# Stick-breaking attention on one core: the second score product of a tile reads 64 rows instead of 128

## The chip, the core and the metric

The kernel runs as one launch on one core of a Trainium2 chip. The metric is the device time of the launch in microseconds. TensorE (PE in the profile; its weight loads are PEld) multiplies matrices, VectorE (DVE), ScalarE (ACT) and GpSimd (POOL) work elementwise, and SyncE (SP) issues the transfers between device memory and the core's own memory.

## The reference

One layer of an encoder: a stick-breaking attention over 2048 positions with 16 heads of 64 channels, then a SwiGLU feed-forward part of width 2816, each between RMS norms with a modulation that comes from a conditioning vector. What matters here is how the scores are made and used:

```python
qkv = (h @ w_qkv).reshape(b, s, 3, N_HEADS, HEAD_DIM)
q, k, v = qkv[:, :, 0], qkv[:, :, 1], qkv[:, :, 2]
for q0 in range(0, s, SB_BLOCK):
    end = q0 + SB_BLOCK
    z = jnp.einsum('bthd,bshd->bhts', q[:, q0:end], k[:, :end]).astype(jnp.float32) * scale
    ...
    sp = jnp.where(mask, jax.nn.softplus(z), 0.0)
    rest = lax.cumsum(sp, axis=3, reverse=True)
    log_a = jnp.where(mask, z - rest, -jnp.inf)
    a = jnp.exp(log_a).astype(v.dtype)
    outs.append(jnp.einsum('bhts,bshd->bthd', a, v[:, :end]))
```

The products are wanted in float32 precision. The kernel gets it by splitting each operand into a rounded high part and a low part, the remainder, and by adding up products of these parts.

## The kernel before, in words

**Stages.** From 0 to about 84 us the first norms and projections are made. From there to about 1391 us attention runs, interleaved with the projections of later heads. Then come the output projection and the feed-forward part; the change touches nothing in them.

**Units of attention.** Heads are taken in 8 pairs `p`, the head within the pair is `e`. Queries and keys are cut into 4 blocks of 512 positions. A unit is (`p`, `e`, query block `qb`, key block `sc`) with `sc` from `qb` down to 0, 160 units in all (L485), and each unit has four tiles `r` of 128 queries by up to 512 keys: 640 tiles. On the diagonal (`sc == qb`) a tile is only (r + 1) x 128 keys wide, so that 64 tiles each are 128, 256 and 384 wide, and the rest are 512 wide.

**Queries and keys in memory.** `project` (L376) makes keys, queries and values of a pair and a block, each as 24 products of 128 rows by 512 columns (L155 to L157), and `split` (L420) puts the high and the low part of the result beside each other into a tile `qn` or `kn`, with the pair's two heads in the two halves of the 128 rows. Transfers then arrange these for the scores. The tile `kt` holds, for each head `e`, the keys' high part in rows 0 to 63 and their low part in rows 64 to 127 (L437 to L441). The tile `qt` holds, for each head, high and low part beside each other in the free dimension, and that twice, in rows 0 to 63 and again in rows 64 to 127 (L450 to L455). One pair and block, `PARKED`, is projected early, kept in device memory and fetched back by `unpark` (L358) with the same layout.

**A score tile.** `score` (L511) makes two products into one accumulator: part 0 takes the queries' high part in all 128 rows and so adds high x high and high x low; part 1 takes the queries' low part in all 128 rows and adds low x high and low x low. The queries are the operand that is loaded (LDWEIGHTS), the keys the one that streams, up to 512 columns wide.

**What follows a tile.** `sigmoids` (L525, ScalarE) reads the accumulator twice, `break_sticks` (L541) scans it on VectorE and multiplies on GpSimd, `turn` (L565) transposes on TensorE, `split_high` and `split_low` (L575, L583) split the transposed weights, and `weigh_values` (L590) multiplies them with the values.

**Order.** TensorE, ScalarE, VectorE and GpSimd run in an order written out by hand (`ORDER_IN_SLOT`): one slot per tile, in which the values' products of the tile nine slots earlier come first, then the two score products of this tile, then one or two slices of a later projection (three products each), and in every second slot two sets of transposes. How many slices a slot gets is reckoned in advance (`RATE`, L1093 to L1097). Transfers all stand in SP's queue, in the order of the program.

Of the kernel before, what the change touches and what calls it, by code (L numbers as in the profile page):

```python
# [16 lines left out]
P = 128  # L17
# [4 lines left out]
HD = 64  # L22
# [59 lines left out]
def f32(ap):  # L82
    return ap.bitcast(F32)
# [3 lines left out]
def hybrid_trunk_kernel(  # L87
# [40 lines left out]
    q_park = dram.tile([P, 2, BT], F32, name="q_park")  # L128
# [42 lines left out]
    def sb(shape, dtype, **kw):  # L171

        return (odd if kw["tag"] in ODD_TAGS else att).tile(shape, dtype, **kw)
# [184 lines left out]
    def unpark():  # L358
        p, b = PARKED
        kt = sb([P, 2, BT], F32R, name=f"kt{p}_{b}", tag="kt", bufs=BUFS["kt"])  # L360
        for e in range(2):
            for part in range(2):
                nc.sync.dma_start(
                    f32(kt[part * HD : (part + 1) * HD, e]), k_park[e * HD : (e + 1) * HD, part]
                )
        qt = sb([P, 2, 2, BT], F32R, name=f"qt{p}_{b}", tag="qt", bufs=BUFS["qt"])
        for e in range(2):
            for half in range(2):
                nc.sync.dma_start(
                    f32(qt[half * HD : (half + 1) * HD, e]), q_park[e * HD : (e + 1) * HD]  # L370
                )
        v = sb([P, 4, 2, 2, HD], F32R, name=f"v{p}_{b}", tag="v", bufs=BUFS["v"])
        nc.sync.dma_start(f32(v), v_park)
        keys[p, b], queries[p, b], values[p, b] = kt, qt, v

    def project(at):  # L376
# [6 lines left out]
        if STEPS[at] == (PARKED[0], 1):  # L383
            unpark()
        h = norm_h[b] if p == 0 or parked else h_load(p, b)

        def product(t):
            if begun:
                return first_acc[t]
            w = weights[p, t]  # L390
            if parked and t == 1:
                acc = zps.tile([P, BT], F32, name=f"pj{p}_{b}_{t}", tag="z")
            else:
                acc = accps.tile([P, BT], F32, name=f"pj{p}_{b}_{t}", tag="acc")
            ahead = b == NB - 1 and p + 1 < NPAIR
            for k in range(KC):
                if t == 1:
                    if p == 0:
                        first_norm(b, k + 3)
                    if k == 0 and nb and nb > 1:  # L400
                        x_load(nb)
                    if k == 5 and waiting:
                        waiting.pop()()
                if parked and t == 1 and k % 2 == 0:
                    nc.sync.dma_start(*stores[k // 2])
                if parked and (t, k) == (1, 6):
                    split_early(1, 2, ["whl"])
                if t == 0 and nb:
                    (x_square if k < 4 else x_scale)(nb, k % 4)
                if t == 2 and k in (2, 4, 6):  # L410
                    first_norm(nb, k // 2 - 1)
                if ahead and k == 0:
                    load_weights(p + 1, t)
                if ahead and k == 6:
                    split_weights(p + 1, t)
                mm3(acc, (w[0][:, k], w[1][:, k]), (h[k][:, 0], h[k][:, 1]), k == 0, k == KC - 1)
                yield
            return acc

        def split(acc, tag):  # L420
            hl = sb([P, 2, BT], F32R, name=f"{tag}n{p}_{b}", tag="qkn", bufs=BUFS["qkn"])
            nc.scalar.copy(hl[:, 0], acc)
            nc.vector.tensor_tensor(hl[:, 1], acc, f32(hl[:, 0]), op=ALU.subtract)
            return hl
# [5 lines left out]
        n = split((yield from product(1)), "k")  # L430
# [13 lines left out]
        n = split((yield from product(0)), "q")  # L444
        if closing:
            wo_load(0, 3, "whl")
        if parked:
            nc.sync.dma_start(q_park, f32(n))
        else:
            qt = sb([P, 2, 2, BT], F32R, name=f"qt{p}_{b}", tag="qt", bufs=BUFS["qt"])  # L450
            for e in range(2):
                for half in range(2):
                    nc.sync.dma_start(
                        f32(qt[half * HD : (half + 1) * HD, e]), f32(n[e * HD : (e + 1) * HD])
                    )  # L455
            queries[p, b] = qt

# [35 lines left out]
    def projections():  # L493
        for at in range(len(STEPS)):
            yield from project(at)
# [15 lines left out]
    def score(i, r):  # L511

        p, e, qb, sc = units[i]
        q, k = queries[p, qb], keys[p, sc]
        diag = sc == qb
        n = (r + 1) * P if diag else BT
        z = zps.tile([P, BT], F32, name=f"z{i}_{r}", tag="z")
        for part in range(2):
            nc.tensor.matmul(  # L519
                z[:, :n], q[:, e, part, r * P : (r + 1) * P], k[:, e, :n],  # L520
                start=part == 0, stop=part == 1,
            )
        scores[i, r] = z
# [490 lines left out]
    def beside_out(b, n):  # L1014
# [40 lines left out]

    stages = {
        "score": score, "sig": sigmoids, "stick": break_sticks,
        "turn": turn, "high": split_high, "low": split_low, "av": weigh_values,
    }
# [7 lines left out]
    for s in range(4 * len(units) + last):  # L1067
        if s % 4 == 0 and s // 4 < len(units):
            p, e, qb, sc = units[s // 4]
# [327 lines left out]
    for n, (s, f) in enumerate(groups):  # L1397
# [3 lines left out]
        for at, product in enumerate(PRODUCTS):  # L1401
            acc = banks_of[{1: 0, 6: 0, 7: 0, 4: 0, 5: 1, 3: 1, 2: 2}[product]]
            for k in range(H4):
                hl, r = left[n - (n == FC), product], right[s, product, k]
# [129 lines left out]
    for m, (at, s, i) in enumerate(out_steps):  # L1534
        product = OUT_PRODUCTS[at]
        acc = bank("y", m % 4, f"o{m}")
        for g in range(GO):
            part, at_part = (0, g) if g < GQ else (1, g - GQ)
            hl, r = left_out[m][part][:, :, at_part], right_out[at, g]
# [61 lines left out]
```

## Time and profile before

| | |
|---|---|
| median of three timed runs | 2849.48 us (2848.0 to 2850.19) |
| profiled execution, its time | 2847.31 us |
| profiled execution, span from first to last instruction | 2845.1 us |
| granted TensorE clock | 0.999 |
| first and last load of the scores | 84.2 and 1391.3 us |
| products of the scores (L519) | 1280, of them 896 are 512 wide and 128 each 384, 256 and 128 wide |

The profile is taken from one execution. It lists busy time by engine; the span in 40 slices; the chain of work that ended last, followed back from the end; and groups of instructions with their count, total and mean duration, and the idle time before them. A row such as `L519 PE MATMUL z<-kt,qt 128*128 128x512 f32 x896 | 281.8, 396 | 0.0` reads: line 519, a product on TensorE into tile z from kt and qt, weights of 128 rows by 128 columns, output of 128 by 512, 896 of them, 281.8 us busy in all, 396 ns from start to modelled end of one, no idle time before them. Products overlap on TensorE, so the distance between starts is less than the duration. In the order of time, the first two columns are start and length of a group of like instructions, in us.

### The profile page before, as it was taken

Reading aid. Unit: us, or ns where it says so; the run is one execution under the profiler, and the core shown is the slowest. Engines: PE = TensorE matmul, PEld = TensorE weight load, DVE = VectorE, ACT = ScalarE, POOL = GpSimd, SP = SyncE. Lnnn points to the kernel's source line nnn. Section 1 sums busy time; section 2 is a strip of 40 time slices with the busy share of each in tenths; the row PEclk is TensorE's granted clock in tenths of the full one; section 3 lists DMA queues with packets and bytes.
Section 4 is the critical chain, followed back from the end, with each engine's and each line's share of the span. In section 5 each row is a group of like instructions: output and inputs, shape, how many; then the busy total and the mean of one; then the engine's idle time right before and its main releaser. Section 6 shows DMA issues by size and latency. Waiting matters only on the chain.

```text
span 2845.1 us, 41790 instructions
## 1 busy us (share of the span) xinstructions
PE 2795.6 (98%) x13848; PEld 2333.9 (82%) x13848; DVE 2028.4 (71%) x2822; ACT 1632.3 (57%) x3265; POOL 1277.0 (45%) x2032
## 2 busy tenths in 40 slices
PE   7999999999999999999999999999999999999998
PEld 6788888888888888887888888888788888888887
DVE  6788898888888888888866766555775665133467
ACT  5787877788787877777645533333433333322243
POOL 1475666676576655656410122221222222544454
PEclk9999999999999999999999999999999999999999
DMA  8765556656665635546289645435453335545566
GB/s 329 271 211 167 189 155 227 211 170 234 189 209 192 209 118 179 196 133 231 88 299 312 203 137 152 122 98 161 130 177 108 112 107 163 191 142 155 180 214 195
DMA packets 239368, 516.84 MB, mean 182 GB/s; under 512 B 22321, under 2 KB 110385, under 8 KB 221489
## 3 DMA queue, kind: packets, MB, share of 16 engines
q1 hardware_dynamic: 239152, 514.18, 56.0%
q8 instruction: 109, 1.79, 0.3%
q14 instruction: 107, 0.87, 0.1%
HBM read 346.85 MB, written 118.49 MB: 164 GB/s over the span
## 4 chain that ended last, share of the span: by engine, by line
PE 87%; DVE 6%; ACT 2%; DMA 2%; issue 2%; POOL 1%; SPq 0%; DVEq 0%; POOLq 0%; ACTq 0%
PE s L155 9%; PE s L156 9%; PE s L157 9%; PE z L519 8%; PE o L598 8%; PE t L570 8%; PE pj L155 6%; PE pj L156 6%; PE pj L157 6%; PE o L156 4%; PE o L157 4%; PE o L155 4%; PE y L157 2%; PE y L155 2%; PE y L156 2%
## 5 line engine op out<-in xcount | busy, mean ns | idle before, releaser
L560 POOL TENSOR_TENSOR a<-a,w 128x512 f32<-128x512 f32 (+3 forms) x640 | 619.4, 968 | 217.8 <-DVE w L553 126.8
L553 DVE TENSOR_TENSOR_SCAN w<-z,c,begin 128x512 f32<-128x512 f32 x384 | 489.6, 1279 | 81.2 <-ACT z L538 61.5
L155 PE MATMUL s<-r,l 128*128 128x512 f32 x1232 | 481.4, 391 | 4.3 <-DVE p L1364 3.7
L157 PE MATMUL s<-r,l 128*128 128x512 f32 x1232 | 479.4, 389 | 0.0
L156 PE MATMUL s<-r,l 128*128 128x512 f32 x1232 | 479.3, 389 | 0.0
L536 ACT ACTIVATE a<-z 128x512 f32<-128x512 f32 (+3 forms) x640 | 347.2, 543 | 167.2 <-PE z L519 135.7
L598 PE MATMUL o<-aT,v 128*128 128x512 f32 (+3 forms) x1280 | 384.3, 381 | 0.1
L586 DVE TENSOR_TENSOR aT<-t,aT 128x512 fp32r<-128x512 f32 (+3 forms) x640 | 359.3, 596 | 22.9 <-ACT aT L580 22.2
L519 PE MATMUL z<-kt,qt 128*128 128x512 f32 (+3 forms) x1280 | 363.1, 365 | 0.0
L580 ACT CAST aT<-t 128x512 fp32r<-128x512 f32 (+3 forms) x640 | 314.1, 533 | 73.5 <-PE t L570 63.5
L538 ACT ACTIVATE z<-z 128x512 f32<-128x512 f32 (+3 forms) x640 | 344.8, 539 | 0.0
L1372 POOL TENSOR_TENSOR one<-p,p 128x512 f32<-128x512 f32 x44 | 70.5, 1602 | 577.8 <-issue 320.5
L155 PE MATMUL pj<-ht,w 128*128 128x512 f32 x768 | 309.7, 403 | 7.6 <-ACT ht L705 2.6
L156 PE MATMUL pj<-ht,w 128*128 128x512 f32 x768 | 302.0, 393 | 1.2 <-DVE ht L710 0.7
L570 PE MATMUL t<-begin,a 128*128 128x128 f32 x2176 | 294.8, 273 | 8.5 <-DVE aT L586 7.2
L570 PEld LDWEIGHTS t<-begin,a 128*128 128x128 f32 x2176 | 255.1, 140 | 58.0 <-DVE aT L586 10.8
L157 PE MATMUL pj<-ht,w 128*128 128x512 f32 x768 | 302.1, 393 | 0.0
L155 PEld LDWEIGHTS s<-r,l 128*128 128x128 f32 x1232 | 231.3, 188 | 54.4 <-ACT l L1225 2.9
L157 PEld LDWEIGHTS s<-r,l 128*128 128x128 f32 x1232 | 231.3, 188 | 48.2
L156 PEld LDWEIGHTS s<-r,l 128*128 128x128 f32 x1232 | 231.3, 188 | 47.9 <-issue 0.5
L548 DVE TENSOR_TENSOR_SCAN w<-z,begin 128x128 f32<-128x128 f32 (+3 forms) x256 | 208.8, 818 | 75.0 <-ACT z L538 62.2
L519 PEld LDWEIGHTS z<-kt,qt 128*128 128x128 f32 x1280 | 230.3, 188 | 37.4 <-DVE w L548 0.2
(160 smaller groups left out, 4865.8 us busy)
## 6 DMA issues: line engine op xcount, KB each, us to landing
ht<-h_s SPq DMA_DIRECT2D x108, 1024.0 KB, 8.1
wi<-in_win SPq DMA_DIRECT2D x86, 512.0 KB, 4.0
qt<-qn SPq DMA_DIRECT2D x124, 256.0 KB, 4.8
ol_qt<-act_s SPq DMA_DIRECT2D x56, 512.0 KB, 3.7
act_s<-S SPq DMA_DIRECT2D x66, 256.0 KB, 4.1
br<-in_wout SPq DMA_DIRECT2D x66, 256.0 KB, 3.6
h_s<-ht SPq DMA_DIRECT2D x16, 1024.0 KB, 7.8
o_s<-os SPq DMA_DIRECT2D x128, 128.0 KB, 2.4
```

What stands on the lines that cost most here:

```text
L155: nc.tensor.matmul(acc, lhs[0], rhs[0], start=first, stop=False, **kw)
L156: nc.tensor.matmul(acc, lhs[0], rhs[1], start=False, stop=False, **kw)
L157: nc.tensor.matmul(acc, lhs[1], rhs[0], start=False, stop=last, **kw)
L519: nc.tensor.matmul(z[:, :n], q[:, e, part, r * P : (r + 1) * P], k[:, e, :n], start=part == 0, stop=part == 1,)
L536: nc.scalar.activation(a[:, :n], z[:, :n], AF.Sigmoid, scale=QK_SCALE)
L538: nc.scalar.activation(z[:, :n], z[:, :n], AF.Sigmoid, scale=-QK_SCALE)
L553: nc.vector.tensor_tensor_scan(rest[:, rev], left[:, rev], begin[:, :BT][:, rev], initial=carries[r], op0=ALU.mult, op1=ALU.bypass,)
L560: nc.gpsimd.tensor_tensor(a[:, :n], a[:, :n], rest[:, 1 : n + 1], op=ALU.mult)
L570: nc.tensor.transpose(pt[:, rb * P : (rb + 1) * P], weighed[i, rb][:, j * P : (j + 1) * P], ident)
L580: nc.scalar.copy(hl[:, 0, t0:], pt[:, t0:])
L586: nc.vector.tensor_tensor(hl[:, 1, t0:], pt[:, t0:], f32(hl[:, 0, t0:]), op=ALU.subtract)
L598: nc.tensor.matmul(acc[:, t0:], lhs, hl[:, part, t0:], start=sc == qb and j == 0 and part == 0, stop=sc == 0 and j == 3 and part == 1,)
```

## The change

The second product of each score tile (part 1, the queries' low part) reads rows 0 to 63 alone, where the keys' high part lies. It leaves out low x low, which the product of 128 rows added. Its output keeps its size. The transfers that fill rows 64 to 127 of `qt` bring the high part only, half of what they brought: in `project` from `qn`, and in `unpark` from device memory. The rest of the tile stays unwritten and unread. The line of the score products becomes L523.

```diff
@@ unpark
                 nc.sync.dma_start(
-                    f32(qt[half * HD : (half + 1) * HD, e]), q_park[e * HD : (e + 1) * HD]
+                    f32(qt[half * HD : (half + 1) * HD, e, : 2 - half]),
+                    q_park[e * HD : (e + 1) * HD, : 2 - half],
                 )
@@ project
                     nc.sync.dma_start(
-                        f32(qt[half * HD : (half + 1) * HD, e]), f32(n[e * HD : (e + 1) * HD])
+                        f32(qt[half * HD : (half + 1) * HD, e, : 2 - half]),
+                        f32(n[e * HD : (e + 1) * HD, : 2 - half]),
                     )
@@ score
-        for part in range(2):
+        for part, rows in enumerate((slice(0, P), slice(0, HD))):
             nc.tensor.matmul(
-                z[:, :n], q[:, e, part, r * P : (r + 1) * P], k[:, e, :n],
+                z[:, :n], q[rows, e, part, r * P : (r + 1) * P], k[rows, e, :n],
                 start=part == 0, stop=part == 1,
             )
```

## The prediction, as put on record before the run

> **What bounds the kernel now.** I read the page first: busy shares, clock, chain.
>
> ```profile
> span 2845.1 us, 41790 instructions
> PE 2795.6 (98%) x13848; PEld 2333.9 (82%) x13848; DVE 2028.4 (71%) x2822; ACT 1632.3 (57%) x3265; POOL 1277.0 (45%) x2032
> PEclk9999999999999999999999999999999999999999
> PE 87%; DVE 6%; ACT 2%; DMA 2%; issue 2%; POOL 1%; SPq 0%; DVEq 0%; POOLq 0%; ACTq 0%
> ```
>
> TensorE is busy for 98% of the span at an undiminished clock, and 87% of the chain that ended last is its own work. The profiled execution took 2847.31 us, so 2.2 us lie around the span; the median of the three timed runs, 2849.48, is 0.08% above it. All sums below start from 2847.31.
>
> Second, the stage that the change touches. All scores are made between 84.2 and 1391.3 us, so I asked for the busy time of each engine before, in and after that window, and then for the scores' line alone in it.
>
> ```profile
> 84.20:1391.30 1307.10, 1288.82 (x7105) 1089.73 (x7104) 1124.12 (x1466) 1029.08 (x2169) 830.62 (x1718) 1.00 0.58 187
> 84.20:1391.30 1307.10, 362.46 (x1279) 230.09 (x1280) 1.00 0.58 187
> ```
>
> The first row is PE, PEld, DVE, ACT, POOL: of 1307.1 us TensorE idles 18.3, VectorE 183.0, ScalarE 278.0. The second row is line 519: 1280 products, two for each of 640 score tiles. So a time added on TensorE here ends up in the span nearly whole, until some 183 us have been added, and beyond that too, since the other engines' work does not grow.
>
> Third, what TensorE waits for in this window (its waits, longest first).
>
> ```profile
> PE t L570 <- DVE aT L586: 7.2, 14, 1.2
> PE pj L155 <- issue: 1.4, 1, 1.4
> PE pj L155 <- DVE qn L423: 1.4, 1, 1.4
> PE xT L315 <- DVE xn L306: 1.2, 4, 0.3
> ```
>
> No transfer is in that list: TensorE never waits for the queries' copies.
>
> Fourth, the sizes of one product, from the groups of this window with shapes kept apart.
>
> ```profile
> L519 PE MATMUL z<-kt,qt 128*128 128x512 f32 x896 | 281.8, 396 | 0.0
> L156 PE MATMUL pj<-ht,w 128*128 128x512 f32 x703 | 275.7, 392 | 0.6 <-DVE ht L333 0.6
> L519 PE MATMUL z<-kt,qt 128*128 128x128 f32 x128 | 22.6, 258 | 0.0
> L519 PEld LDWEIGHTS z<-kt,qt 128*128 128x128 f32 x1280 | 230.3, 188 | 37.4 <-DVE w L548 0.2
> ```
>
> The reader is to see the "128*128": every product in this kernel, scores and all others, stands with 128 rows of weights. A score product lasts 396 ns from its start to its modelled end, and its load 188.
>
> Fifth, how these lie beside each other (order of time around 800 us, first the products, then the loads).
>
> ```profile
> 800.95 0.63 PE L519 MATMUL z<-kt,qt 128*128 128x512 f32 x2
> 801.42 0.39 PE L155 MATMUL pj<-ht,w 128*128 128x512 f32 x1
> 801.65 0.40 PE L156 MATMUL pj<-ht,w 128*128 128x512 f32 x1
> 801.88 0.39 PE L157 MATMUL pj<-ht,w 128*128 128x512 f32 x1
> 802.11 0.33 PE L598 MATMUL o<-aT,v 128*128 128x128 f32 x2
> 802.28 0.68 PE L519 MATMUL z<-kt,qt 128*128 128x512 f32 x2
> ```
>
> ```profile
> 801.19 0.19 PEld L155 LDWEIGHTS pj<-ht,w 128*128 128x128 f32 x1
> 801.42 0.19 PEld L156 LDWEIGHTS pj<-ht,w 128*128 128x128 f32 x1
> 801.65 0.19 PEld L157 LDWEIGHTS pj<-ht,w 128*128 128x128 f32 x1
> 804.25 0.30 PEld L598 LDWEIGHTS o<-aT,v 128*128 128x128 f32 x2
> ```
>
> Products 512 wide start 0.23 us apart (801.42, 801.65, 801.88) though each lasts 0.39: the next streams in while the last 0.16 of the one before is still on its way out. The load of the product that starts at 801.65 starts at 801.42, together with the product before it: loads lie wholly under streaming. Where two loads stand back to back (the 804.25 row, 0.30 for two of 0.19) the second starts 0.11 after the first, so 0.11 is what a load occupies. Two products only 128 wide take 0.17 from start to next start (802.11 to 802.28): 0.06 for the first, whose successor was already loaded, and 0.11 for the second, behind which the next load is late.
>
> **The change part by part.** No engine's order moves: the built program has the same sequence on PE, DVE, ACT and POOL, and on SP the same transfers, of which a few neighbours change places; only shapes differ.
>
> (a) The 640 second products read 64 rows of queries and keys in place of 128. Their width stays, and streaming is by width: the 128-wide products above start 0.06 apart and the 512-wide ones 0.23, a factor of four. So the products themselves save nothing: 0.
>
> (b) The upper half of the queries' tile no longer gets the low part.
>
> ```profile
> L453 SPq DMA_DIRECT2D qt<-qn x124: 461/596/2084, 52.9 to 1317.4; - x124
> qt<-qn SPq DMA_DIRECT2D x124, 256.0 KB, 4.8
> ```
>
> 62 of these 124 copies, and two of the four from the parked copy, go from 256 to 128 KB: 64 x 128 KB = 8.4 MB of the page's 517. They are still issued, at the same 0.6 us each on SP, and TensorE waited for none of them. Worth 0; the cover is that projections run ahead of the scores.
>
> (c) What is new is height. Around each second product TensorE goes from 128 rows to 64 and back: 2 x 640 = 1280 switches, each between neighbours that today overlap twice, in load and in drain. No row of before shows a product of another height, so I bound a switch from both sides. Least: slightly below 0 if a 64-row load takes less time (below, the faster rival). Most: the product before runs out fully and only then is the load begun and waited for, 0.16 + 0.19 = 0.35 us, 1280 x 0.35 = 448 us. Between them: the load no longer goes under the product before but is done in the open, 0.11, while the last 0.16 of the old product runs out beside it.
>
> I take 0.11, because it is the nearest row: where the trace does show a product whose load could not be hidden (behind a 128-wide one), the gap grew to 0.11 and not to 0.35. The sum: 1280 x 0.11 = 140.8 us. On the 64 tiles that are 128 wide (128 products in the group above) the load behind the second product is in the open already, 0.11 instead of 0.06, which takes off 64 x 0.05 = 3.2. Of the 18.3 us of idle time I count nothing as absorbed, since most of it waits for chains that move along with TensorE. 2847.31 + 137.6 = **2985 us**, 4.8% slower.
>
> Two rules of the Trainium skill bear on (c), on opposite sides. "TensorE: Matmul & The Clock Gate", section LDWEIGHTS, says that the time of a load goes by its columns and not by its rows; no run here shows 64 rows yet, and by it (a) and the loads bring nothing. "TensorEngine Tiling (Array Packing)", section Key Properties, says that "Changing tiling mode (not just tile) drains the TensorE". By that rule each switch would cost at least the run-out; this is the drain rival below, and no row of before can confirm it.
>
> (d) What is late next. If TensorE loses 0.22 us per tile, a tile's slot goes from 1307.1 / 640 = 2.04 us to 2.26. ScalarE, VectorE and GpSimd then have more slack per slot, so no new engine binds; queues and pools keep their order. No wait is added: the second score product has none of its own, and those who read the scores (ScalarE's two sigmoids) come 0.11 later per tile with slack to spare.
>
> **The rivals.**
>
> Drain: before each change of height the array runs out, then loads. For it: the trace shows two overlaps of neighbours, and a change of shape may end both. Against it: nothing shows that a load cannot run during the run-out. Price 0.16 to 0.35 per switch, 205 to 448 us: 3052 to 3295; fully in sequence 3295. Between 0.11 and 0.16 it shades into the forecast.
>
> Small bubble: only a short stop, of the order of one narrow product's 0.06 (a choice: the shortest interval between two products above): 1280 x 0.06 = 77 us, 2924, and less for a shorter one.
>
> No cost (the other side): 64 rows are just a mask on the same array, the load goes under the product before as now, and the change does in effect nothing on TensorE. It decides at zero exposed time per switch: from 5.7 us in total, 4 ns a switch, it would be slower. For it: loads are hidden today with 0.23 - 0.11 = 0.12 to spare. Time 2847.
>
> Faster: a 64-row load occupies half, 0.055. It then helps only where a load is in the open, ahead of a narrow product's successor, at most 64 x 0.055 = 3.5 us. To this comes the pair of wide scores, which takes 0.47 from start to next start (800.95 to 801.42) or 0.235 each, against 0.23: 640 x 0.005 = 3.2 us if that excess goes with the rows. Together some 7 us: 2840.
>
> **How the numbers follow.** Forecast (0.06 to 0.19 per switch, 0.19 being a whole load: 2924 to 3090) 0.34; drain above that 0.22; small bubble, up to 2924, 0.18; no cost 0.16; faster 0.10. A measurement of this kernel can tell about 0.2% from no change, 5.7 us. So slower 0.74, same 0.16, faster 0.10. Ends of the range: the high one is the full price of a switch, 3295, since the row that prices it is as real as the one I chose; the low one 2841, which takes in the no-cost case and leaves the faster one out. The likeliest case's own range is 2924 to 3090; the whole is wide because one unknown per switch is multiplied by 1280.
>
> **What would show it.** In the changed kernel the second products should stand as a form of their own with 64 rows. By the forecast, starts from a first score product to its second, and from the second to what follows, lie near 0.34 apart instead of 0.23, with the load of a switch beginning when the product before has streamed and not with it, while pairs elsewhere (three projection products in a row) stay at 0.23; the window of the scores grows by about 138 us and what follows it stays at 1453.8 (2845.1 - 1391.3). By the drain rival the starts lie 0.39 to 0.58 apart and each switch's load begins after the modelled end of the product before. By the no-cost rival the starts stay at 0.23 and the window at 1307. That only one of the two directions costs, which would halve the sum (2916), is what I would least like to have missed; the starts into and out of the 64 rows tell it. If time shows up outside the window, or on another engine, the reasoning is wrong altogether.

## The result and the profile after

The changed kernel takes 3078.47 us (median of four runs, 3076.56 to 3081.76) against 2849.05 before: ratio 1.0804, 95% interval 1.0791 to 1.0816. That is 229 us more, where 138 were forecast. The profiled execution took 3078.48 us.

The page of the changed kernel, the lines that answer to those of before:

```profile
span 3076.4 us, 41812 instructions
PE 3035.9 (99%) x13848; PEld 2314.2 (75%) x13848; DVE 2046.0 (67%) x2822; ACT 1646.1 (54%) x3265; POOL 1278.2 (42%) x2032
PEclk9999999999999999999999999999999999999999
PE 90%; DVE 4%; DMA 2%; issue 1%; ACT 1%; POOL 1%; SPq 0%; DVEq 0%; POOLq 0%; ACTq 0%
```

TensorE has the same 13848 products and 240 us more busy time at the same clock; the others have nearly what they had (VectorE 18 us more, ScalarE 14, GpSimd 1). The busy time of the loads, PEld, has not grown (2333.9 before, 2314.2 now): the loads themselves have not become longer.

The stages, cut at the first and the last score (columns as before; the last score now starts at 1620.4):

```profile
84.20:1620.00 1535.80, 1527.41 (x7105) 1069.12 (x7104) 1143.14 (x1466) 1043.18 (x2171) 831.80 (x1719) 1.00 0.48 154
1620.00:3076.40 1456.40, 1440.47 (x6405) 1188.88 (x6404) 851.31 (x1257) 556.41 (x1028) 437.48 (x295) 1.00 0.53 168
```

The scores' window has grown from 1307.1 to 1535.8 us, by 228.7, and holds the loss but for some 3 us: what follows takes 1456.4 against 1453.8. TensorE's idle time in the window has gone from 18.3 to 8.4 us: a slower TensorE waits less for its operands.

Where in the window? The groups of TensorE there, shapes kept apart; the first row is L155 before the change, the other four are the changed kernel:

```profile
L155 PE MATMUL pj<-ht,w 128*128 128x512 f32 x703 | 282.0, 401 | 5.0 <-issue 1.4 <-DVE qn L423 1.4 <-ACT hf L325 0.9
```

```profile
L155 PE MATMUL pj<-ht,w 128*128 128x512 f32 x703 | 335.5, 477 | 3.8 <-DVE qn L424 1.4 <-ACT hf L325 0.9 <-PE vt L469 0.8
L156 PE MATMUL pj<-ht,w 128*128 128x512 f32 x703 | 277.3, 394 | 0.1
L523 PE MATMUL z<-kt,qt 64*128 64x512 f32 x448 | 222.3, 496 | 0.0
L523 PE MATMUL z<-kt,qt 128*128 128x512 f32 x448 | 179.1, 400 | 0.0
```

The second score products stand as a form of their own, "64*128", and last 496 ns from start to end instead of some 400. The other row that has grown is L155, the first projection product after the scores, from 401 ns before to 477 in the mean, though nothing in it was changed; L156, one further, is as it was. Both grown rows sit right behind a change of height: in the trace 543 of the 640 second score products are followed by L155, the rest by other products of 128 rows. (The shape after the weights' is that of the operand that streams, 64 by 512 here, and not that of the output, which keeps its 128 rows.)

The loads of the same window, again L155 before the change first:

```profile
L155 PEld LDWEIGHTS pj<-ht,w 128*128 128x128 f32 x702 | 132.2, 188 | 28.7 <-DVE qn L423 1.8 <-issue 1.6 <-ACT hf L325 1.2
```

```profile
L155 PEld LDWEIGHTS pj<-ht,w 128*128 128x128 f32 x702 | 131.0, 187 | 121.0 <-issue 98.4 <-DVE qn L424 1.8 <-ACT hf L325 1.2
L523 PEld LDWEIGHTS z<-kt,qt 128*128 128x128 f32 x640 | 120.6, 188 | 19.4
L523 PEld LDWEIGHTS z<-kt,qt 64*128 64x128 f32 x640 | 117.1, 183 | 191.4 <-issue 189.7
```

A load of 64 rows takes 183 ns, as good as one of 128. But ahead of it the load unit idles, 191.4 us in 640 times, 0.30 each; ahead of the first score load of a tile it idles 0.03. Ahead of L155 the idle time has gone from 28.7 to 121.0 us. "issue" means that the profile shows nothing that it waited for: no semaphore and no transfer.

And the order of time around 900 us, products first, then loads. A group stands under the shape of its first product; the two of L523 are the one of 128 rows and the one of 64.

```profile
905.11 0.81 PE L523 MATMUL z<-kt,qt 128*128 128x512 f32 x2
905.85 0.50 PE L155 MATMUL pj<-ht,w 128*128 128x512 f32 x1
```

```profile
904.99 0.19 PEld L523 LDWEIGHTS z<-kt,qt 128*128 128x128 f32 x1
905.42 0.18 PEld L523 LDWEIGHTS z<-kt,qt 64*128 64x128 f32 x1 [0.25 <-issue]
905.85 0.19 PEld L155 LDWEIGHTS pj<-ht,w 128*128 128x128 f32 x1 [0.24 <-issue]
905.96 0.19 PEld L156 LDWEIGHTS pj<-ht,w 128*128 128x128 f32 x1
```

This is where the time goes. The first score product starts at 905.11 and has streamed by 905.34 (0.23 for 512 columns). Before the change the load of the second would have begun at about 905.11, under it. Now it begins at 905.42: not during the streaming, and not at its end either, but 0.08 after. It occupies 0.11, so the second product streams from 905.53 to 905.76; then again 0.09 pass before the projection's load begins at 905.85. The load behind that, at 905.96, lies under its predecessor as ever: 0.11 after the load before it. So each change of height costs a stop of 0.08 to 0.09 us and then a load of 0.11 in the open, 0.2 in all, in both directions alike. (A product's start is recorded when its load begins here, which is why L155 shows 0.50: load and product.)

These rows are typical. Counted from the end of streaming in the same way, the stop is 0.09 us in the median at all 1280 changes, never under 0.08, whether the product before is 128 or 512 wide and whichever line follows. From the start of a tile's first score product to the start of the second product behind the pair, the 448 tiles 512 wide take 1.085 us (median) against 0.693 before the change, 0.196 per change of height; the tiles 384 and 256 wide lose 0.39 each as well, and the tiles 128 wide 0.29. Over all 640 tiles that is 244 us. The window grew by 229, or 0.18 per change: 10 us went into idle time that TensorE had anyway, and some 5 stay open. What the stop itself is made of, no run here shows.

### The profile page after: what moved, and what is told of

The parts are those of the page before. It is cut to its first block, busy times and chain, and to the rows that moved or that the text cites. A ratio compares the mean times of both kernels' runs of the same rounds, so it can differ in the third digit from the quotient of the medians.

```text
span 3076.4 us, 41812 instructions
## 1 busy us (share of the span) xinstructions
PE 3035.9 (99%) x13848; PEld 2314.2 (75%) x13848; DVE 2046.0 (67%) x2822; ACT 1646.1 (54%) x3265; POOL 1278.2 (42%) x2032
## 4 chain that ended last, share of the span: by engine, by line
PE 90%; DVE 4%; DMA 2%; issue 1%; ACT 1%; POOL 1%; SPq 0%; DVEq 0%; POOLq 0%; ACTq 0%
PE z L523 12%; PE pj L155 9%; PE s L155 9%; PE s L157 9%; PE s L156 9%; PE o L602 8%; PE t L574 8%; PE pj L156 5%; PE pj L157 5%; PE o L155 4%; PE o L156 4%; PE o L157 4%; PE y L155 1%; PE y L157 1%; PE y L156 1%
## 5 line engine op out<-in xcount | busy, mean ns | idle before, releaser
L155 PE MATMUL s<-r,l 128*128 128x512 f32 x1232 | 482.1, 391 | 4.3 <-DVE p L1368 3.9
L523 PE MATMUL z<-kt,qt 128*128 128x512 f32 (+7 forms) x1280 | 484.9, 414 | 0.0
L156 PE MATMUL s<-r,l 128*128 128x512 f32 x1232 | 479.8, 389 | 0.0
L523 PEld LDWEIGHTS z<-kt,qt 128*128 128x128 f32 (+1 forms) x1280 | 237.7, 186 | 210.9 <-issue 189.7
L155 PE MATMUL pj<-ht,w 128*128 128x512 f32 x768 | 363.3, 473 | 6.4 <-ACT ht L709 2.6
L156 PE MATMUL pj<-ht,w 128*128 128x512 f32 x768 | 303.7, 395 | 0.8 <-DVE ht L714 0.7
L157 PE MATMUL pj<-ht,w 128*128 128x512 f32 x768 | 302.6, 394 | 0.0
L155 PEld LDWEIGHTS s<-r,l 128*128 128x128 f32 x1232 | 231.7, 188 | 54.4 <-ACT l L1229 2.9
L156 PEld LDWEIGHTS s<-r,l 128*128 128x128 f32 x1232 | 231.7, 188 | 48.5 <-issue 0.5
```

What stands on the lines that cost most here:

```text
L155: nc.tensor.matmul(acc, lhs[0], rhs[0], start=first, stop=False, **kw)
L156: nc.tensor.matmul(acc, lhs[0], rhs[1], start=False, stop=False, **kw)
L157: nc.tensor.matmul(acc, lhs[1], rhs[0], start=False, stop=last, **kw)
L523: nc.tensor.matmul(z[:, :n], q[rows, e, part, r * P : (r + 1) * P], k[rows, e, :n], start=part == 0, stop=part == 1,)
```

## The experiments

**Theory:** the price hangs on a change of height between neighbours on TensorE, about 0.18 us for each. **Rivals:** every product of 64 rows pays, whoever its neighbours are; the smaller copies cost or gain; the stop grows with the difference in height; any change of shape pays. Each ratio is to the kernel before, timed on the same chip as the run; the changes of height are counted in the traces. The two adjacent runs have 18 more than two per tile, because nine values' products and nine score products of 64 rows have no partner of their height beside them.

| run | changes of height | median us | ratio, 95% interval | us more than before, per change |
|---|---|---|---|---|
| the change | 1280 | 3078.47 | 1.0804 (1.0791 to 1.0816) | 0.179 |
| full copies | 1280 | 3076.50 | 1.0804 (1.0786 to 1.0822) | 0.178 |
| both scores 64 | 1280 | 3082.82 | 1.0818 (1.0802 to 1.0834) | 0.183 |
| 32 rows | 1280 | 3077.75 | 1.0800 (1.0784 to 1.0816) | 0.179 |
| odd tiles | 640 | 2965.93 | 1.0411 (1.0395 to 1.0426) | 0.183 |
| apart | 2560 | 3319.29 | 1.1656 (1.1636 to 1.1676) | 0.184 |
| adjacent | 1298 | 3082.08 | 1.0821 (1.0803 to 1.0839) | 0.179 |
| adjacent, upper half | 1298 | 2976.11 | 1.0444 (1.0429 to 1.0460) | - |
| 64 columns | 0 | 2846.93 | 0.9993 (0.9983 to 1.0002) | - |

**Full copies.** The height alone, the transfers as before. The edit is shown against the changed kernel.

```diff
-                    f32(qt[half * HD : (half + 1) * HD, e, : 2 - half]),
-                    q_park[e * HD : (e + 1) * HD, : 2 - half],
+                    f32(qt[half * HD : (half + 1) * HD, e]), q_park[e * HD : (e + 1) * HD]
...
-                        f32(qt[half * HD : (half + 1) * HD, e, : 2 - half]),
-                        f32(n[e * HD : (e + 1) * HD, : 2 - half]),
+                        f32(qt[half * HD : (half + 1) * HD, e]), f32(n[e * HD : (e + 1) * HD])
```

> The changed kernel with the queries' copies back at full size, so that only the height of the second product is changed. If the whole loss comes from the height: as the changed kernel, 3078 us, within 0.2%. Rival (the smaller copies cost time, by their different pieces or their place in SP's queue): nearer to 2849 us. If the smaller copies had gained something, above 3084 us.

It measured 3076.50 us, the same ratio 1.0804. The copies are worth nothing that these runs can tell, in either direction. Their rows do change: with full size there are 124 of 256 KB at 4.4 us to landing; in the changed kernel half of them are smaller and land sooner, and TensorE waits for none of them in either:

```profile
qt<-qn SPq DMA_DIRECT2D x62, 256.0 KB, 3.8
qt<-qn SPq DMA_DIRECT2D x62, 128.0 KB, 3.3
```

**Both scores 64.** Twice the products of 64 rows, as many changes of height.

```diff
-        for part, rows in enumerate((slice(0, P), slice(0, HD))):
+        for part, rows in enumerate((slice(0, HD), slice(0, HD))):
```

> Both score products of a tile take 64 rows; this leaves out the queries' high part with the keys' low part. 1280 products of 64 rows, but still only 2 changes of height per tile. Theory (a price of about 0.18 us per change of height): 3078 us, and the start of the second product comes 0.23 us after the first, its load under the first. Rival (each product of 64 rows pays, because a load of 64 rows is never done ahead): twice the loss, 2849 + 2 x 229 = 3307 us, with 0.33 us or more between the two starts.

It measured 3082.82 us, not 3307: the rival that charges each product of 64 rows falls. The loads of this run in order of time:

```profile
1201.11 0.30 PEld L602 LDWEIGHTS o<-aT,v 128*128 128x128 f32 x2
1201.78 0.29 PEld L523 LDWEIGHTS z<-kt,qt 64*128 64x128 f32 x2 [0.36 <-issue]
1202.44 0.19 PEld L155 LDWEIGHTS pj<-ht,w 128*128 128x128 f32 x1 [0.37 <-issue]
```

The two loads of 64 rows stand back to back, 0.29 for both, the second 0.11 after the first and ahead of its own product: among equals, 64 rows are loaded ahead like any others. The idle time stands before the first of them and before the projection's load, at the changes. One detail of the expectation was off: the starts of the two score products lie not 0.23 but 0.34 apart, since the first now carries the open load (0.11 + 0.23). That is the number that the rival gave as its sign, but not for the rival's reason: the second load lies only 0.11 behind the first.

**32 rows.** A larger difference in height.

```diff
-        for part, rows in enumerate((slice(0, P), slice(0, HD))):
+        for part, rows in enumerate((slice(0, P), slice(0, 32))):
```

> The second score product takes 32 rows; this leaves out the low part's products of half the channels. Theory (a fixed stop of about 0.08 us after streaming and a load of 0.11 in the open, at each change): 3078 us. Rival (the stop is the time that the difference in height takes to run out, so it grows by half from 64 to 96 rows): 0.04 more per change, 1280 x 0.04 = 51, near 3130 us. Rival (a shorter load for fewer rows): below 3050 us.

It measured 3077.75 us. Between 64 and 32 rows neither the stop nor the load depends on how far the height changes; the group of loads has 181 ns each and the same idle time ahead of them:

```profile
L523 PEld LDWEIGHTS z<-kt,qt 32*128 32x128 f32 x640 | 116.0, 181 | 192.1 <-issue 190.4
```

**Odd tiles.** Half as many changes.

```diff
-        for part, rows in enumerate((slice(0, P), slice(0, HD))):
+        for part, rows in enumerate((slice(0, P), slice(0, HD if r % 2 else P))):
```

> Only tiles 1 and 3 of a unit's four take 64 rows in the second product, copies at full size. 640 changes of height in place of 1280. Theory: half the loss, 2849 + 115 = 2964 us. Rival (part of the loss comes only when TensorE falls behind in every slot, and idle time would absorb single ones): clearly less than half, below 2940 us.

It measured 2965.93 us, half the loss within 2 us. The price is paid singly, not only by a TensorE that is late in every slot.

**Apart, and adjacent.** The sharpest pair: the second values' product is narrowed as well, and then the two score products of a tile are merely exchanged, which brings the two narrowed products together.

```diff
-        for part in range(2):
+        for part, rows in enumerate((slice(0, P), slice(0, HD))):
             nc.tensor.matmul(
-                acc[:, t0:], lhs, hl[:, part, t0:],
+                acc[:, t0:], lhs[rows], hl[rows, part, t0:],
```

> The changed kernel, and the second values' product too reads 64 of its 128 rows; this leaves out half of the weights' low part. Per slot the order is values 128, values 64, scores 128, scores 64, projection 128: four changes of height. Theory (a price per change): 2849 + 2 x 229 = 3307 us.

```diff
-        for part, rows in enumerate((slice(0, P), slice(0, HD))):
+        for part, rows in ((1, slice(0, HD)), (0, slice(0, P))):
             nc.tensor.matmul(
                 z[:, :n], q[rows, e, part, r * P : (r + 1) * P], k[rows, e, :n],
-                start=part == 0, stop=part == 1,
+                start=part == 1, stop=part == 0,
```

> The same products as the run with both narrowed, only the two of a score tile in the other order, so that per slot it goes values 128, values 64, scores 64, scores 128, projection 128: two changes of height with the same 1280 products of 64 rows. Theory (price per change): 3078 us, 229 less than with the products apart. Rival (price per product of 64 rows): the same as apart, 3307 us.

Apart 3319.29 us, adjacent 3082.08: 237 us between two kernels with the same products, the same loads and the same bytes, in another order. The exchange of the two score products takes the changes of height from 2560 to 1298, which is 0.188 us for each of the 1262 that are gone. The loads of the adjacent run show where the stops have gone:

```profile
1202.15 0.19 PEld L602 LDWEIGHTS o<-aT,v 128*128 128x128 f32 x1
1202.59 0.18 PEld L602 LDWEIGHTS o<-aT,v 64*128 64x128 f32 x1 [0.24 <-issue]
1202.69 0.19 PEld L523 LDWEIGHTS z<-kt,qt 64*128 64x128 f32 x1
1203.25 0.19 PEld L523 LDWEIGHTS z<-kt,qt 128*128 128x128 f32 x1 [0.37 <-issue]
1203.36 0.19 PEld L155 LDWEIGHTS pj<-ht,w 128*128 128x128 f32 x1
```

The stop ahead of L155 is gone (it follows 0.11 behind a load of its own height), and there is none between the two loads of 64 rows. The two that are left stand where the height changes. Whole groups say the same: 164.3 us of "issue" ahead of the values' 64 rows, 2.3 ahead of the scores' 64 rows, 189.3 ahead of the scores' 128.

```profile
L523 PEld LDWEIGHTS z<-kt,qt 128*128 128x128 f32 x640 | 119.2, 186 | 191.9 <-issue 189.3 <-DMA ht<-h_s 0.2 <-DMA kt<-kn 0.2
L523 PEld LDWEIGHTS z<-kt,qt 64*128 64x128 f32 x640 | 119.1, 186 | 3.1 <-issue 2.3 <-DVE w L552 0.4 <-DVE ht L333 0.4
L602 PEld LDWEIGHTS o<-aT,v 64*128 64x128 f32 x640 | 117.0, 183 | 173.1 <-issue 164.3 <-DVE xr L894 0.4 <-DVE x_ms L846 0.4
```

**Adjacent, upper half.** The values' product moves to rows 64 to 127, the scores' stays in rows 0 to 63.

```diff
-        for part, rows in enumerate((slice(0, P), slice(0, HD))):
+        for part, rows in enumerate((slice(0, P), slice(HD, P))):
             nc.tensor.matmul(
                 acc[:, t0:], lhs[rows], hl[rows, part, t0:],
```

> As the adjacent run, but the values' product of 64 rows reads rows 64 to 127 and the scores' one after it rows 0 to 63, into different accumulators. If products of different halves of the rows run side by side: up to a whole 512-wide product less per slot, 640 x 0.2 = 130, near 2950 us. If they only queue: as the adjacent run, 3078 us. If a change of the half is a change of shape as well: a third one per slot, 3078 + 115 = 3193 us.

It measured 2976.11 us, 106 less than the adjacent run, 0.166 per slot; forecast were 130, counted as if each slot won 0.2. A pair can win no more than its narrower product: over the 631 pairs that is 379 columns in the mean, 0.17 us at 0.23 for 512, or 107 us in all, and 106 were measured. The third option falls: to pass from one half to the other is no change of shape. Products, then loads:

```profile
1200.92 0.44 PE L602 MATMUL o<-aT,v 64*128 64x384 f32 x1
1200.92 0.92 PE L523 MATMUL z<-kt,qt 64*128 64x512 f32 x2
```

```profile
1200.92 0.18 PEld L602 LDWEIGHTS o<-aT,v 64*128 64x128 f32 x1 [0.31 <-issue]
1200.92 0.18 PEld L523 LDWEIGHTS z<-kt,qt 64*128 64x128 f32 x1
1201.34 0.19 PEld L523 LDWEIGHTS z<-kt,qt 128*128 128x128 f32 x1 [0.24 <-issue]
```

Both loads and both products of 64 rows start together at 1200.92, and the next load at 1201.34 comes 0.42 later, which is a load, one product 512 wide and a stop (0.11 + 0.23 + 0.08): the second product of the pair took no time of its own. In the trace 630 of the 631 pairs start together like this. Even so the slot loses: two changes cost about 0.36 and the pair returns 0.17. The Trainium skill, "TensorE: Matmul & The Clock Gate", section "Part 3: Packing small matmuls — row/col tiling", describes such neighbours in different row groups as running side by side; this run agrees.

**64 columns.** The other dimension of the loaded weights, on the kernel before, with all heights at 128.

```diff
-                acc[:, t0:], lhs, hl[:, part, t0:],
+                acc[: P - HD * part, t0:], lhs[:, : P - HD * part], hl[:, part, t0:],
                 start=sc == qb and j == 0 and part == 0, stop=sc == 0 and j == 3 and part == 1,
+                skip_group_check=True,
```

> The kernel before, with another narrowing: the second values' product of a tile (the weights' low part) takes only the 64 columns of the values' high part and writes 64 rows of the accumulator; it leaves out low x low. Heights all stay 128; the width of the loaded weights changes 1280 times. Theory, if any change of the array's shape has the price of a change of height: near 3078 us. Rival (only rows count): 2849 us, or a little less, since a load goes by its columns and some loads stand in the open behind narrow products.

It measured 2846.93 us, ratio 0.9993 with an interval that takes in 1. The rival that any change of the loaded shape pays falls: 1280 changes between 128 and 64 columns cost nothing. The loads are shorter, 136 ns against 189, and next to no idle time of "issue" stands before them (0.5 us in all):

```profile
L598 PEld LDWEIGHTS o<-aT,v 128*128 128x128 f32 x640 | 121.2, 189 | 14.7 <-ACT os L605 0.4 <-ACT a L536 0.2 <-ACT z L538 0.2
L598 PEld LDWEIGHTS o<-aT,v 128*64 128x64 f32 x640 | 87.1, 136 | 13.9 <-issue 0.5
```

No run beat the kernel before clearly. No run has two narrow products in different halves of the columns, so whether these would run side by side is not shown.

## Why the prediction came out as it did

**The bound** was read rightly: TensorE in this stage, nothing to cover it. 228.7 of the loss lie in the scores' window, where no other engine's busy time grew by more than 19 us (VectorE).

**(a) The products save nothing:** right. 64 rows load as long as 128 (183 and 188 ns) and stream as long: in the run with both scores at 64 rows the load after a pair comes 0.66 after the pair's first, 0.11 + 2 x 0.23 + 0.09.

**(b) The copies are worth 0:** right, by the run with full copies, 1.0804 in both.

**(c) The price of a change of height** is the term that was mis-sized. I took 0.11 per change, the load in the open, and let the run-out of the product before lie beside it. It measured 0.18 in the time and 0.2 in the rows, because ahead of the open load there stands a stop of 0.08 to 0.09 that I had put at nothing. On the tiles 128 wide the loss was 0.10 smaller than on the others, where I had taken off 0.05. The row that I called nearest, the gap of 0.11 behind a 128-wide product, is a load that is late for want of cover; it cannot show a stop, since no neighbour there differs in height. The forecast's own range, 0.06 to 0.19, holds the value near its upper end, and that is partly luck: 0.19 was the recorded length of a load, with no stop in it. The direction and the place, open loads on both sides of each second product, were right: the load behind a change begins after streaming, as the forecast said, and all 1280 changes pay, none in one direction only.

**The drain rival** had more truth than its 0.22. Its prices begin at 0.16, 3052 us, so 3078 lies in its range as well as in the forecast's, and the time alone does not choose between them. By the rows each has a part. From streaming to streaming it is 0.42 to 0.44 us into and out of the 64 rows (the recorded starts, 0.33 and 0.42 apart, count the first only to the load), where the forecast said 0.34 and the rival 0.39 to 0.58. But the load waits after streaming only 0.08 to 0.09 and not 0.16 (it begins at 905.42, before the modelled end 905.51 of the product that started at 905.11 and lasted 0.40), and then it is paid too. Since ends of products are modelled, whether the array is empty by then stays open. "TensorEngine Tiling (Array Packing)" of the Trainium skill, section Key Properties, says that changing the tiling mode drains the array. The runs agree that a change of height has a price (apart against adjacent, 237 us), 0.18 us here, without showing that it is a drain. The run with 64 columns changes the columns as often and pays nothing; since a trace shows the rows and columns in use and not the mode, it does not tell whether the rule fails there or the mode stayed the same.

**The small bubble, no cost and faster** are excluded: 0.18 per change against 0.06 at most, 0 and below.

**(d) What is late next:** nothing, as said. TensorE's idle time fell by 10 us, which I had counted as not absorbable; part of it was.

## What to carry to other kernels

Where TensorE is the bound, count the changes of the contraction height between neighbouring products, not the products: here each cost 0.18 us, over a third of a pair of score products (0.47), whether it went from 128 to 64 or 32 rows and back. A product that needs only 64 rows costs no more at 128, so leave the spare rows filled with something harmless, or bring the products of one height together; exchanging two products was worth 237 us in one pair of runs. A load that the profile shows with idle time before it, and with "issue" as the reason, is the sign to look for.

## What the runs showed of the hardware that I had not expected

- The price of a change of height is a stop of 0.08 to 0.09 us and an open load of 0.11, the same in both directions and the same for 32 as for 64 rows (3077.75 and 3078.47 us).
- A change between 128 and 64 loaded columns had no such price (ratio 0.9993, 0.9983 to 1.0002), and its load is shorter, 136 ns against 189.
- Two products of 64 rows in different halves, into different accumulators, start together and cost the time of the wider one (630 of 631 pairs, 106 us less).
